# Sums of weights on VectorE, two score chunks in one PSUM bank, and a second buffer for a first block, in a hybrid FoX and mLSTM layer

## The chip, the cores and the metric

The kernel runs on one core of a Trainium2 chip. The time is that of the device, in microseconds (us), for one execution of the whole layer. Three executions of the kernel before took 957.70, 958.07 and 958.45 us; the median is 958.07 us.

## The reference: what is computed

One layer of a decoder trunk, in float32, for 512 tokens with 16 learned meta tokens put before them (528 rows), width 1024. The input is normalised, one projection gives thirteen pieces, and two branches work on them side by side:

```
h = rms_norm(x, g_pre);  z = h @ w_in
fq, fk, fv, ff, fz, mqk, mv, mi, mf, mo, mz, ga, gb = split(z)
# FoX: 8 heads of 128, causal softmax attention with a decay from cumsum(log_sigmoid(ff))
p  = softmax(where(causal, fq.fk * scale + cum[q] - cum[k], -inf))
ya = ((p @ fv) * silu(fz)) @ w_a
# mLSTM: 4 heads, keys of 256, values of 512, chunks of 128, after a causal convolution of mqk
hb = sigmoid(mo) * mlstm_scan(mq, mk, mv, log_i, log_f)
yb = (rms_norm(hb, g_head) * silu(mz)) @ w_b
merged = sigmoid(ga) * ya + sigmoid(gb) * yb
out = x + rms_norm(merged @ w_o, g_post)      # without the 16 meta rows
```

The widths that matter here: fq, fz, ga and gb are 1024 wide each, mz is 2048.

## The kernel before

**Precision.** Every float32 operand of a matmul is split in a high part, rounded to TensorE's fast float32 form, and a low rest. `mm3` (L148 to L151) makes three matmuls of each product: high by high (L149) and the two mixed ones (L150, L151). The high part of a weight is a copy on ScalarE, the low part a subtraction on VectorE: L141 and L143 in `wsplit`, L249 and L251 in `split`. In the profile's names a tile `wq_r` is the raw weight as loaded, `wq_h` and `wq_l` are its two parts.

**Units of seven products.** For fq, fz, ga, gb and mz, 256 output channels at a time, the kernel multiplies a 2 by 2 block form of the weights and of the tokens with seven block products instead of eight (`st_products`, letters X, Y, Z, W for the quarter of two PSUM banks into which a product goes). `st_narrow` prepares the weights of such a unit: the first block by itself (`wXa`, memory `whs`/`wls` in the pool `sums`, one buffer), then two sums in place on the raw weights by GpSimd (L259 and L260, 128 partitions by 512), the split of these (`wXb`), of the second raw tile (`wXc`), two sums by VectorE (L265, L266) and the split of those (`wXd`). The prefix names the unit: `wz10` is the first of the two z units of mLSTM head 1, `wz11` the second, `wfz0`, `wgb1`, `wga2` and `wfq2` are units of FoX. In a unit the products come in this order: X with a, Y and Z with b, W and Y with c, X and Z with d. ScalarE takes snapshots out of the banks between them: L313 after the first Y, L317 after W, L321 after X. VectorE recombines at the end (L324, L325, L327). There are 8 z units, two for each head, and 16 in FoX: four each of fq, fz, ga and gb.

**The order of the program.** For each of four mLSTM heads: the convolution of q and k, the values, the scores (`score_part`: VectorE L727, ScalarE L728, VectorE L730 and L732), the output gate `so`, and the first pair of value chunks (`value_part`, L785 to L806), the first z unit, the second pair of chunks, the second z unit. Head 0 takes `so` as a plain projection ahead of the scores (sigmoids L741), the others as a wide unit behind them (sigmoids L757). The transposes `pht` (L816), which read the normalised chunks (L806), and the products `pyb` of a head come with the next head. Then come four rounds p = 0 to 3 of FoX, each of two heads: fq, fk, then for each head `prob_part` (scores `pl`, softmax), `ptr_part` (transposes, copies L986 and L987) and `fout_part` (L1005), and between them fv in even rounds and one or two gate units: fz and then gb in p = 0 and p = 2, fz and then gb or ga in p = 1 and p = 3. fz ends with a sigmoid and a multiplication (L920, L921), gb and ga with a sigmoid (L927). At the end stand the merge with w_a and the output projection.

**What sets the order.** A scheduler orders the instructions of each engine ahead of the run, from the program's order, the operations' assumed costs and the buffers that are free; each engine then executes its list strictly in that order. Buffers come from pools with a fixed number of turns: four for raw weights, four each for `wXb`, `wXc`, `wXd` and the other split weights together, eight PSUM banks, one for `whs` and `wls`. A tile waits until the last reader of its predecessor in that buffer is done. Loads stand in SyncE's list, and every raw tile is a load of 512 KB.

Of the kernel before, what the change touches and what calls it, by code (L numbers as in the profile page):

```python
# [26 lines left out]
MV = 512  # L27
# [5 lines left out]
C_MO, C_MZ, C_GA, C_GB = 8208, 10256, 12304, 13328  # L33
# [8 lines left out]
OFFA = [0, 144, 416, 816]  # L42
# [11 lines left out]
def tile_hybrid_block(ctx: ExitStack, tc: tile.TileContext, x, meta, norm_pre, norm_post, w_in, b_fox_f,  # L54
# [14 lines left out]
    def psum1(name):  # L69
        return pa.tile([P, 512], F32, tag="pa", name=name)  # L70
# [22 lines left out]

    wk = ctx.enter_context(tc.tile_pool(name="work", bufs=1))
    mw = ctx.enter_context(tc.tile_pool(name="sums", bufs=1))

    def sb(shape, dt, tag, name, pool=None, **kw):

# [143 lines left out]
        TB["b21"] = blk(hh, 1, 0), blk(hl, 1, 0)  # L242
        TB["b22"] = blk(hh, 1, 1), blk(hl, 1, 1)

    def split(src, name, tags=("whi", "wlo"), pool=None, bufs=None):
        kw = {} if bufs is None else {"bufs": bufs}
        shape = [P, src.shape[1], src.shape[2]]
        hi = (pool or wp).tile(shape, F32R, tag=tags[0], name=f"{name}_h", **kw)
        S.activation(hi, src, AF.Copy)  # L249
        lo = (pool or wp).tile(shape, F32R, tag=tags[1], name=f"{name}_l", **kw)  # L250
        V.tensor_tensor(lo, src, f(hi), ALU.subtract)  # L251
        return hi, lo

    def st_narrow(c0, name):

        (r0,), (r1,) = (wload(win, 512 * i, 4, c0, 256, f"{name}{i}")[0] for i in range(2))
        a, b = slice(0, P), slice(P, 2 * P)
        o = {"a11": split(r0[:, :, a], f"{name}a", ("whs", "wls"), mw, 1)}
        G.tensor_tensor(r0[:, :, a], r0[:, :, a], r0[:, :, b], ALU.add)  # L259
        G.tensor_tensor(r0[:, :, b], r0[:, :, b], r1[:, :, b], ALU.add)  # L260
        x, y = split(r0, f"{name}b")
        o["s3"], o["s1"] = (x[:, :, a], y[:, :, a]), (x[:, :, b], y[:, :, b])
        x, y = split(r1, f"{name}c")
        o["a12"], o["a22"] = (x[:, :, a], y[:, :, a]), (x[:, :, b], y[:, :, b])
        V.tensor_tensor(r1[:, :, b], r0[:, :, a], r1[:, :, b], ALU.add)  # L265
        V.tensor_tensor(r1[:, :, a], r1[:, :, a], r1[:, :, b], ALU.add)  # L266
        x, y = split(r1, f"{name}d")
        o["s4"], o["s2"] = (x[:, :, a], y[:, :, a]), (x[:, :, b], y[:, :, b])
        return o
# [18 lines left out]
    def st_products(o, units):  # L288


        begun = set()

        def prod(d, w, t):
            (wh_, wl_), (th, tl) = o[w], TB[t]
            for m, (wz, yx, _, ts) in enumerate(units):
                bank = wz if d in "WZ" else yx
                dst = bank[:, 0:256] if d in "WY" else bank[:, 256:512]
                first = (m, d in "WZ") not in begun
                begun.add((m, d in "WZ"))
# [12 lines left out]
        for wz, yx, snap, _ in units:
            S.activation(snap[:, 0:2], halves(yx), AF.Copy)  # L313
        prod("Z", "s1", "t1")
        prod("W", "a12", "b21")
        for wz, yx, snap, _ in units:
            S.activation(snap[:, 3], wz[:, 256:512], AF.Copy)  # L317
        prod("Y", "a22", "t4")
        prod("X", "s2", "t2")
        for wz, yx, snap, _ in units:  # L320
            S.activation(snap[:, 2], yx[:, 256:512], AF.Copy)  # L321
        prod("Z", "s4", "b22")
        for wz, yx, snap, _ in units:
            V.tensor_tensor(yx[:, 256:512], snap[:, 0], yx[:, 256:512], ALU.subtract)  # L324
            V.tensor_tensor(halves(yx), halves(yx), snap[:, 2:4], ALU.subtract)  # L325
        for wz, yx, snap, _ in units:
            V.tensor_tensor(halves(wz), halves(wz), snap[:, 1:3], ALU.add)  # L327
# [177 lines left out]
    for b in range(NCH):  # L505
# [6 lines left out]
        s0 = NM + b * P  # L512
# [244 lines left out]
                S.activation(dst, units[m][i].rearrange("p (s n) -> p s n", s=2), AF.Sigmoid)  # L757
        return so

    def st_unit(c0, name, room):  # L760

        ps = banks(f"p{name}", 2)
        st_products(st_narrow(c0, f"w{name}"), [(ps[0], ps[1], room.rearrange("p a (b n) -> p (a b) n", b=2), None)])
        return ps

    def mz_part(h, u):
        g = sb([P, 2, SEQ], F32, ("qk1h", "qk1l")[u], f"gz{h}{u}")
        ps = st_unit(C_MZ + h * MV + u * 256, f"z{h}{u}", g)
        for m in range(2):
            S.activation(g[:, m, :], ps[m], AF.Sigmoid)  # L770
        for m in range(2):
            mi = 80 + h * 4 + u * 2 + m
            V.scalar_tensor_tensor(g[:, m, :], ps[m], gc[:, mi:mi + 1], g[:, m, :], ALU.mult, ALU.mult)
        return g
# [165 lines left out]
    def prob_part(p, m, q, k):  # L940

        h = 2 * p + m
        qh, ql = q
        kh, kl = k
        ab = sb([P, NA], F32, "ab", f"ab{h}", gp)
        nc.sync.dma_start(ab, d_na[h:h + 1, :].to_broadcast([P, NA]))
        pn = sb([P, NPACK], F32, "w", f"pn{h}")
        for c in range(NCH):
            kn = NM + (c + 1) * P
            o = OFFA[c] + kn - P  # L950
            G.tensor_tensor(ab[:, o:o + P], ab[:, o:o + P], mask_q, ALU.add)
            lt = sb([P, L], F32, "y", f"lt{h}{c}", bufs=2)
            parts = [(0, kn)] if kn <= 512 else [(0, HL), (HL, kn)]
            mn = line(wk, f"mn{h}{c}", 2, tag="mn", bufs=4)
            for i, (s0, s1) in enumerate(parts):
                ps = psum1(f"pl{h}{c}{i}")
                mm3(ps[:, 0:s1 - s0], qh[:, m, c * P:(c + 1) * P], ql[:, m, c * P:(c + 1) * P],
                    kh[:, m, s0:s1], kl[:, m, s0:s1], True, True)
                V.tensor_tensor_reduce(out=lt[:, s0:s1], in0=ps[:, 0:s1 - s0], in1=ab[:, OFFA[c] + s0:OFFA[c] + s1],
                                       op0=ALU.add, op1=ALU.min, scale=1.0,  # L960
                                       scalar=3e38 if i == 0 else mn[:, 0:1], accum_out=mn[:, i:i + 1])
            li = len(parts) - 1
            rsum = line(wk, f"rsum{h}{c}", 1, tag="r", bufs=4)
            S.activation(lt[:, 0:kn], lt[:, 0:kn], AF.Exp, bias=mn[:, li:li + 1], scale=-1.0, accum_out=rsum)
            V.reciprocal(rsum, rsum)  # L965
            o = OFFP[c]
            G.tensor_scalar(pn[:, o:o + P].rearrange("p (g t) -> p g t", g=4),  # L967
                            lt[:, 0:32].unsqueeze(1).to_broadcast([P, 4, 32]), rsum, None, ALU.mult)
            V.tensor_scalar(pn[:, o + P:o + P + kn - NM], lt[:, NM:kn], rsum, None, ALU.mult)
        return pn  # L970

    def ptr_part(p, m, pn):
        h = 2 * p + m
        pth = sb([P, NCH, SEQ], F32R, "big_h", f"pth{h}")
        ptl = sb([P, NCH, SEQ], F32R, "big_l", f"ptl{h}")
        ptm = sb([P, SEQ], F32R, "ptm", f"ptm{h}", gp)
        pmt = psum1(f"pmt{h}")
        for c in range(NCH):
            o = OFFP[c]
            pt = psum1(f"pt{h}{c}")  # L980
            for j in range(c + 1):
                T.transpose(pt[:, j * P:(j + 1) * P], pn[:, o + P + j * P:o + P + (j + 1) * P], ident)
            T.transpose(pmt[:, c * P:(c + 1) * P], pn[:, o:o + P], ident)
            pv = pt[:, 0:(c + 1) * P].rearrange("p (j t) -> p j t", t=P)
            dst = pth[:, 0:c + 1, c * P:(c + 1) * P]
            S.activation(dst, pv, AF.Copy)  # L986
            V.tensor_tensor(ptl[:, 0:c + 1, c * P:(c + 1) * P], pv, f(dst), ALU.subtract)  # L987
# [28 lines left out]
        return gh, gl  # L1016

    bt = turn_part(*pend)
    gp = ctx.enter_context(tc.tile_pool(name="fox", bufs=1))
    d_yb = [dram.tile([P, 2, SEQ], F32, name=f"d_yb{u}") for u in range(4)]  # L1020
    d_sa = [dram.tile([P, 2, SEQ], F32, name=f"d_sa{u}") for u in range(3)]
    q = fq_part(0)
# [138 lines left out]
```

## Time and profile before

| | us |
|---|---|
| median of three executions | 958.07 |
| the profiled execution | 958.12 |
| its span, first to last instruction | 956.3 |
| TensorE (PE) busy | 915.8 (96%) |
| VectorE (DVE) busy | 649.0 (68%) |
| ScalarE (ACT) busy | 473.9 (50%) |
| GpSimd (POOL) busy | 194.1 (20%) |
| mean granted TensorE clock | 0.999 |

The profiled execution took 1.8 us more than its span. TensorE works almost without a pause, so the times at which it stands and what it then waits for say more than the shares of the other engines. In the views an entry such as "PE pz L149 <- ACT gz L317" says that the matmul of line 149 into tile pz waited for ScalarE's instruction of line 317 on tile gz. In a timeline each row is one instruction or a run of like ones: its start, its length, engine, line, operation, the tile written and those read, shapes, and in brackets the time that the engine stood idle before it with what ended that. Tiles are shown without their numbers: `pz` is any of the z units' banks.

### The profile page before, as it was taken

The page shows a single profiled execution, that of the slowest core. Times are in us where ns is not written, and L with a number is a line of the kernel's source. Part 1 is how long each engine was busy: PE and PEld are TensorE (multiplying, and loading weights), DVE is VectorE, ACT ScalarE, POOL GpSimd, SP SyncE. Part 2 cuts the span into 40 slices and gives each one's busy share as a digit, 9 for nine tenths or more (in the row PEclk, how much of TensorE's full clock was granted, in tenths as well). Part 3 has the DMA queues.
Part 4 walks back from the last instruction along what each step waited for, and adds up shares of the span by engine and source line. Part 5 has one row for each costly group of instructions (what it writes and reads, how often), then busy time and mean ns, then how long its engine had stood idle before and what let it go on. Part 6 is the DMA issues. An engine that isn't in the chain of part 4 may idle for free.

```text
span 956.3 us, 15752 instructions
## 1 busy us (share of the span) xinstructions
PE 915.8 (96%) x6296; PEld 844.5 (88%) x6296; DVE 649.0 (68%) x1080; ACT 473.9 (50%) x818; POOL 194.1 (20%) x222
## 2 busy tenths in 40 slices
PE   8999799999999999999999999989899999899997
PEld 6998799889998899988999988889798899798887
DVE  6988598447686276872768665677774676885633
ACT  5746456435565254662545424455653554773331
POOL 3055100120101211012112114223531233410000
PEclk9999999999999999999999999999999999999999
DMA  7323143203223222322223325224342233248402
GB/s 226 91 82 95 45 129 104 88 23 111 88 90 105 61 81 75 113 77 87 73 61 110 112 88 162 62 79 133 102 155 74 73 90 110 89 167 311 145 23 89
DMA packets 73539, 97.47 MB, mean 102 GB/s; under 512 B 5237, under 2 KB 56533, under 8 KB 73466
## 3 DMA queue, kind: packets, MB, share of 16 engines
q1 hardware_dynamic: 71400, 92.76, 31.7%
q0 software_dynamic: 576, 2.10, 0.6%
q10 hardware_dynamic: 1490, 1.61, 0.5%
q8 instruction: 49, 0.80, 0.3%
q14 instruction: 24, 0.20, 0.1%
HBM read 90.62 MB, written 5.83 MB: 101 GB/s over the span
## 4 chain that ended last, share of the span: by engine, by line
PE 73%; DVE 11%; issue 5%; POOL 5%; ACT 4%; DMA 1%; POOLq 0%; DVEq 0%; ACTq 0%
PE pyb L150 3%; PE pyb L151 3%; PE pyb L149 3%; PE pv L151 3%; PE pv L150 3%; PE pv L149 3%; PE po L149 3%; PE po L151 3%; PE po L150 3%; PE pqk L149 3%; PE pqk L151 3%; PE pqk L150 3%; PE pfk L149 2%; PE pfk L151 2%; PE pfk L150 2%
## 5 line engine op out<-in xcount | busy, mean ns | idle before, releaser
L967 POOL TENSOR_SCALAR pn<-lt,rsum 128x128 f32<-128x128 f32 x32 | 31.1, 972 | 108.6 <-DVE rsum L965 58.6
L150 PE MATMUL pyb<-bl,wb_h 128*128 128x512 f32 x128 | 49.9, 390 | 0.0
L151 PE MATMUL pyb<-bh,wb_l 128*128 128x512 f32 x128 | 49.8, 389 | 0.0
L149 PE MATMUL pyb<-bh,wb_h 128*128 128x512 f32 x128 | 49.8, 389 | 0.0
L150 PE MATMUL pv<-wv_l,hh 128*128 128x512 f32 (+1 forms) x128 | 46.6, 364 | 1.5 <-DVE wv_l L143 1.5
L151 PE MATMUL pv<-wv_h,hl 128*128 128x512 f32 (+1 forms) x128 | 46.4, 363 | 0.0
L149 PE MATMUL pv<-wv_h,hh 128*128 128x512 f32 (+1 forms) x128 | 46.4, 363 | 0.0
L694 DVE SCALAR_TENSOR_TENSOR y<-z,gc,y 128x512 f32<-128x512 f32 (+1 forms) x48 | 36.2, 759 | 2.0 <-ACT y L687 1.3
L149 PE MATMUL pqk<-hh,wq_h 128*128 128x258 f32 x128 | 36.4, 284 | 0.0
L149 PE MATMUL pfk<-hh,wfk_h 128*128 128x264 f32 x128 | 36.4, 284 | 0.0
L149 PE MATMUL pqk<-hh,wk_h 128*128 128x264 f32 x128 | 36.3, 284 | 0.0
L151 PE MATMUL pqk<-hh,wk_l 128*128 128x264 f32 x128 | 36.3, 284 | 0.0
L150 PE MATMUL pfk<-hl,wfk_h 128*128 128x264 f32 x128 | 36.3, 284 | 0.0
L151 PE MATMUL pfk<-hh,wfk_l 128*128 128x264 f32 x128 | 36.3, 283 | 0.0
L150 PE MATMUL pqk<-hl,wk_h 128*128 128x264 f32 x128 | 36.3, 283 | 0.0
L150 PE MATMUL pqk<-hl,wq_h 128*128 128x258 f32 x128 | 36.0, 282 | 0.0
L151 PE MATMUL pqk<-hh,wq_l 128*128 128x258 f32 x128 | 36.0, 282 | 0.0
L150 PEld LDWEIGHTS pv<-wv_l,hh 128*128 128x128 f32 x128 | 24.1, 189 | 5.6 <-DVE wv_l L143 1.7
L151 PEld LDWEIGHTS pyb<-bh,wb_l 128*128 128x128 f32 x128 | 24.0, 188 | 5.0
L149 PEld LDWEIGHTS pyb<-bh,wb_h 128*128 128x128 f32 x128 | 24.0, 188 | 4.9
L150 PEld LDWEIGHTS pyb<-bl,wb_h 128*128 128x128 f32 x128 | 24.0, 188 | 4.9
L149 PEld LDWEIGHTS pv<-wv_h,hh 128*128 128x128 f32 x128 | 24.2, 189 | 3.9
(1806 smaller groups left out, 3662.1 us busy)
## 6 DMA issues: line engine op xcount, KB each, us to landing
wv_r<-in_w_in_dram SPq DMA_DIRECT2D x16, 512.0 KB, 4.5
wo_r<-in_w_in_dram SPq DMA_DIRECT2D x16, 512.0 KB, 4.1
wz_r<-in_w_in_dram SPq DMA_DIRECT2D x16, 512.0 KB, 3.7
wb_r<-in_w_b_dram SPq DMA_DIRECT2D x16, 512.0 KB, 3.4
ab<-d_na SPq DMA_DIRECT2D x8, 672.0 KB, 3.8
wq_r<-in_w_in_dram SPq DMA_DIRECT2D x8, 512.0 KB, 3.6
wk_r<-in_w_in_dram SPq DMA_DIRECT2D x8, 512.0 KB, 3.7
wfq_r<-in_w_in_dram SPq DMA_DIRECT2D x8, 512.0 KB, 3.6
```

Source lines behind the costliest of these rows:

```text
L149: T.matmul(ps, ah, bh, start=start, stop=False, **kw)
L150: T.matmul(ps, ah, bl, start=False, stop=False, **kw)
L151: T.matmul(ps, al, bh, start=False, stop=stop, **kw)
L694: V.scalar_tensor_tensor(y[:, t0:L], z[:, m, t0 + j:L + j], gc[:, j * 16 + mi:j * 16 + mi + 1], y[:, t0:L], ALU.mult, ALU.add)
L967: G.tensor_scalar(pn[:, o:o + P].rearrange("p (g t) -> p g t", g=4), lt[:, 0:32].unsqueeze(1).to_broadcast([P, 4, 32]), rsum, None, ALU.mult)
```

## The change

It has three parts.

1. `st_narrow` is told which engine makes the two sums of L259 and L260. The 16 units of FoX use VectorE, the 8 z units of the mLSTM stay with GpSimd.
2. In `prob_part` the score matmuls of all four chunks of a head are written ahead of the softmax, and the first two chunks go into one PSUM bank, 144 columns of one and 272 of the other behind it. Four banks are used for a head's scores instead of five. In `ptr_part` the copies out of PSUM are written behind all transposes.
3. The first block of the second z unit of each head gets memory of its own, under the name `sg` in the pool `fox`, which is opened at the program's start instead of before FoX. Until then this memory is used by nothing else.

```diff
+    gp = ctx.enter_context(tc.tile_pool(name="fox", bufs=1))
...
-    def split(src, name, tags=("whi", "wlo"), pool=None, bufs=None):
+    def split(src, name, tags=("whi", "wlo"), pool=None, bufs=None, into=None):
...
-        hi = (pool or wp).tile(shape, F32R, tag=tags[0], name=f"{name}_h", **kw)
+        hi = into[0] if into else (pool or wp).tile(shape, F32R, tag=tags[0], name=f"{name}_h", **kw)
         S.activation(hi, src, AF.Copy)
-        lo = (pool or wp).tile(shape, F32R, tag=tags[1], name=f"{name}_l", **kw)
+        lo = into[1] if into else (pool or wp).tile(shape, F32R, tag=tags[1], name=f"{name}_l", **kw)
         V.tensor_tensor(lo, src, f(hi), ALU.subtract)
...
-    def st_narrow(c0, name):
+    def st_narrow(c0, name, adder, into=None):
...
-        o = {"a11": split(r0[:, :, a], f"{name}a", ("whs", "wls"), mw, 1)}
-        G.tensor_tensor(r0[:, :, a], r0[:, :, a], r0[:, :, b], ALU.add)
-        G.tensor_tensor(r0[:, :, b], r0[:, :, b], r1[:, :, b], ALU.add)
+        o = {"a11": split(r0[:, :, a], f"{name}a", ("whs", "wls"), mw, 1, into)}
+        adder.tensor_tensor(r0[:, :, a], r0[:, :, a], r0[:, :, b], ALU.add)
+        adder.tensor_tensor(r0[:, :, b], r0[:, :, b], r1[:, :, b], ALU.add)
...
-    def st_unit(c0, name, room):
+    def st_unit(c0, name, room, adder=V, into=None):
...
     def mz_part(h, u):
         g = sb([P, 2, SEQ], F32, ("qk1h", "qk1l")[u], f"gz{h}{u}")
-        ps = st_unit(C_MZ + h * MV + u * 256, f"z{h}{u}", g)
+        into = None
+        if u:
+            t = sb([P, 2, 4, P], F32R, "sg", f"wz{h}{u}a", gp)
+            into = t[:, 0], t[:, 1]
+        ps = st_unit(C_MZ + h * MV + u * 256, f"z{h}{u}", g, G, into)
...
+        sums = []
         for c in range(NCH):
             kn = NM + (c + 1) * P
             o = OFFA[c] + kn - P
             G.tensor_tensor(ab[:, o:o + P], ab[:, o:o + P], mask_q, ALU.add)
+            for s0, s1 in [(0, kn)] if kn <= 512 else [(0, HL), (HL, kn)]:
+
+                if c != 1:
+                    bank = psum1(f"pl{h}{c}{s0}")
+                ps = (bank[:, 144:512] if c == 1 else bank)[:, 0:s1 - s0]
+                mm3(ps, qh[:, m, c * P:(c + 1) * P], ql[:, m, c * P:(c + 1) * P],
+                    kh[:, m, s0:s1], kl[:, m, s0:s1], True, True)
+                sums.append((c, s0, s1, ps))
...
-            V.tensor_tensor(ptl[:, 0:c + 1, c * P:(c + 1) * P], pv, f(dst), ALU.subtract)
+            pts.append(pt[:, 0:(c + 1) * P].rearrange("p (j t) -> p j t", t=P))
+        for c, pv in enumerate(pts):
```

The order of TensorE's instructions is the same in both. What moves is on the other engines, and three places matter. In the rows the number in front is the row's place in its engine's list; the changed text has other line numbers.

VectorE in mLSTM head 0, between the split of the first z unit's weights (`wz00`) and the head's scores (`w`, `wl`), before:

```order
129 L251 TENSOR_TENSOR wz00c_l<-wz_r_1252,wz00c_h 128x1024
130 L265 TENSOR_TENSOR wz_r_1252<-wz_r_1250,wz_r_1252 128x4x128
131 L266 TENSOR_TENSOR wz_r_1252<-wz_r_1252 128x4x128
132 L251 TENSOR_TENSOR wz00d_l<-wz_r_1252,wz00d_h 128x1024
133 L727 TENSOR_TENSOR w_957<-ps_1120,w_957 128x512
134 L727 TENSOR_TENSOR w_957<-ps_1130,w_957 128x384
135 L730 TENSOR_TENSOR wl_1119<-w_957,wh_1118 128x512
```

and with the change:

```order
129 L252 TENSOR_TENSOR wz00c_l<-wz_r_1255,wz00c_h 128x1024
130 L252 TENSOR_TENSOR wz01a<-wz_r_1428,wz01a 128x512
131 L266 TENSOR_TENSOR wz_r_1255<-wz_r_1253,wz_r_1255 128x4x128
132 L267 TENSOR_TENSOR wz_r_1255<-wz_r_1255 128x4x128
133 L252 TENSOR_TENSOR wz00d_l<-wz_r_1255,wz00d_h 128x1024
134 L728 TENSOR_TENSOR w_960<-ps_1123,w_960 128x512
135 L252 TENSOR_TENSOR wz01b_l<-wz_r_1428,wz01b_h 128x1024
136 L731 TENSOR_TENSOR wl_1122<-w_960,wh_1121 128x512
```

The second z unit's `wz01a` and `wz01b` have come ahead of the scores; before, they stood behind the first pair of value chunks. ScalarE's `wz01b_h` likewise now stands between the sigmoids of `so` (L741 before) and the copies `wh`.

ScalarE in head 1, from the output gate's snapshots to the first z unit's first snapshot (`gz`, L313 before), before:

```order
186 L249 ACTIVATE wz10c_h<-wz_r_2551 128x1024
...
191 L249 ACTIVATE wz10d_h<-wz_r_2551 128x1024
192 L757 ACTIVATE so_2238<-po_0_2239 128x2x256
...
198 L249 ACTIVATE wz11a_h<-wz_r_2723 128x512
199 L313 ACTIVATE gz_2546<-pz_1_2548 128x512
200 L249 ACTIVATE wz11b_h<-wz_r_2723 128x1024
201 L249 ACTIVATE wz11c_h<-wz_r_2725 128x1024
202 L317 ACTIVATE gz_2546<-pz_0_2547 128x256
```

and with the change:

```order
186 L250 ACTIVATE wz11a<-wz_r_2726 128x512
187 L250 ACTIVATE wz10c_h<-wz_r_2553 128x1024
...
192 L250 ACTIVATE wz10d_h<-wz_r_2553 128x1024
193 L250 ACTIVATE wz11b_h<-wz_r_2726 128x1024
194 L758 ACTIVATE so_2240<-po_0_2241 128x2x256
...
200 L314 ACTIVATE gz_2548<-pz_1_2550 128x512
201 L250 ACTIVATE wz11c_h<-wz_r_2728 128x1024
```

The copies of wz11a and wz11b have come ahead of the sigmoids of `so`; only that of wz11c still stands between the two snapshots.

ScalarE in FoX, p = 0, in the fz unit (`yb` and `pfz`) while the weights of the gb unit (`wgb1`) are prepared, before:

```order
475 L313 ACTIVATE yb<-pfz_1_6420 128x512
476 L249 ACTIVATE wgb1b_h<-wgb_r_6589 128x1024
477 L964 ACTIVATE lt_6402,rsum_6414<-lt_6402,mn_6403 128x528
478 L249 ACTIVATE wgb1c_h<-wgb_r_6591 128x1024
479 L317 ACTIVATE yb<-pfz_0_6419 128x256
480 L321 ACTIVATE yb<-pfz_1_6420 128x256
```

and with the change:

```order
475 L314 ACTIVATE yb<-pfz_1_6414 128x512
476 L977 ACTIVATE lt_6404,rsum_6408<-lt_6404,mn_6405 128x528
477 L250 ACTIVATE wgb1b_h<-wgb_r_6583 128x1024
478 L318 ACTIVATE yb<-pfz_0_6413 128x256
479 L250 ACTIVATE wgb1c_h<-wgb_r_6585 128x1024
480 L322 ACTIVATE yb<-pfz_1_6414 128x256
```

The exponential of the softmax stands ahead of wgb1b_h, and the snapshot L317 (now L318) ahead of wgb1c_h.

More of the change, by code (lines that the diff above doesn't have):

```diff
@@ L758, in mo_part @@
         return so
-    def st_unit(c0, name, room):
+    def st_unit(c0, name, room, adder=V, into=None):
         ps = banks(f"p{name}", 2)
-        st_products(st_narrow(c0, f"w{name}"), [(ps[0], ps[1], room.rearrange("p a (b n) -> p (a b) n", b=2), None)])
+        st_products(st_narrow(c0, f"w{name}", adder, into), [(ps[0], ps[1], room.rearrange("p a (b n) -> p (a b) n", b=2), None)])
         return ps
@@ L951, in prob_part @@
             G.tensor_tensor(ab[:, o:o + P], ab[:, o:o + P], mask_q, ALU.add)
+            for s0, s1 in [(0, kn)] if kn <= 512 else [(0, HL), (HL, kn)]:
[5 more added lines that the diff above has]
+                sums.append((c, s0, s1, ps))
+        for c in range(NCH):
+            kn = NM + (c + 1) * P
             lt = sb([P, L], F32, "y", f"lt{h}{c}", bufs=2)
-            parts = [(0, kn)] if kn <= 512 else [(0, HL), (HL, kn)]
             mn = line(wk, f"mn{h}{c}", 2, tag="mn", bufs=4)
[L955 to L959, printed above, removed]
+            parts = [(s0, s1, ps) for c_, s0, s1, ps in sums if c_ == c]
+            for i, (s0, s1, ps) in enumerate(parts):
+                V.tensor_tensor_reduce(out=lt[:, s0:s1], in0=ps, in1=ab[:, OFFA[c] + s0:OFFA[c] + s1],
                                        op0=ALU.add, op1=ALU.min, scale=1.0,
@@ L977, in ptr_part @@
         pmt = psum1(f"pmt{h}")
+        pts = []
         for c in range(NCH):
@@ L983, in ptr_part @@
             T.transpose(pmt[:, c * P:(c + 1) * P], pn[:, o:o + P], ident)
-            pv = pt[:, 0:(c + 1) * P].rearrange("p (j t) -> p j t", t=P)
+            pts.append(pt[:, 0:(c + 1) * P].rearrange("p (j t) -> p j t", t=P))
+        for c, pv in enumerate(pts):
             dst = pth[:, 0:c + 1, c * P:(c + 1) * P]
@@ L1018, in tile_hybrid_block @@
     bt = turn_part(*pend)
-    gp = ctx.enter_context(tc.tile_pool(name="fox", bufs=1))
     d_yb = [dram.tile([P, 2, SEQ], F32, name=f"d_yb{u}") for u in range(4)]
```

## The prediction

> **What bounds the kernel now.** I read the page first, then the clock (0.999, so it plays no part), then TensorE's waits, then the engines' timelines around the long ones.
>
> ```profile
> span 956.3 us, 15752 instructions
> ## 1 busy us (share of the span) xinstructions
> PE 915.8 (96%) x6296; PEld 844.5 (88%) x6296; DVE 649.0 (68%) x1080; ACT 473.9 (50%) x818; POOL 194.1 (20%) x222
> ```
>
> The change leaves every matmul as it is. All that can be won lies in the 956.3 − 915.8 = 40.5 us in which TensorE is idle, and all that can be lost is a longer wait there. TensorE's waits (waiting line and tile, releaser, total in us, times, longest), for 500 to 860 us (FoX), 112 to 525 (mLSTM) and 99 to 103 (head 0's scores):
>
> ```profile
> PE pfz L149 <- ACT yb L317: 6.7, 4, 2.2
> PE pga L149 <- ACT sga L317: 3.6, 2, 2.0
> PE pgb L149 <- DVE yb L921: 3.5, 2, 1.8
> PE pl L149 <- DVE ptl L987: 2.0, 2, 1.0
> PE pgb L149 <- ACT sgb L317: 1.6, 1, 1.6
> PE pl L149 <- DVE mn L959: 1.0, 2, 0.5
> ```
>
> ```profile
> PE pz L149 <- ACT gz L317: 3.5, 7, 0.8
> PE pht L816 <- DVE ht L806: 1.2, 2, 0.6
> PE pz L149 <- ACT gz L313: 0.6, 1, 0.6
> ```
>
> ```profile
> PE ps L149 <- ACT yb L741: 3.2, 1, 3.2
> ```
>
> The L317 and L313 rows are one story: the last products of a seven-product unit write into a PSUM bank of which ScalarE must first have copied the other half. The timelines of ScalarE and GpSimd show why it is late (start, length, engine, line, tiles, idle before it and what ended that), in head 1's z units and in the fz unit of p = 0:
>
> ```profile
> 243.82 1.06 ACT L249 ACTIVATE wz11b_h<-wz_r 128x1024 fp32r<-128x1024 f32 x1 [3.15 <-POOL wz_r L260]
> ```
>
> ```profile
> 620.76 1.06 ACT L249 ACTIVATE wgb1b_h<-wgb_r 128x1024 fp32r<-128x1024 f32 x1 [3.45 <-POOL wgb_r L260]
> ```
>
> ```profile
> 622.45 1.04 ACT L249 ACTIVATE wgb1c_h<-wgb_r 128x1024 fp32r<-128x1024 f32 x1
> 623.39 0.36 ACT L317 ACTIVATE yb<-pfz 128x256 f32<-128x256 f32 x1
> ```
>
> ```profile
> 619.45 1.28 POOL L260 TENSOR_TENSOR wgb_r<-wgb_r,wgb_r 128x512 f32<-128x512 f32 x1
> ```
>
> ScalarE works in order. The copy wX·b (L249) of the *next* unit stands ahead of the snapshot L317 and waits for the GpSimd sums L259 and L260; ScalarE idles 3.15 and 3.45 us, and TensorE waits behind the snapshot.
>
> **The change part by part: the mLSTM.** GpSimd keeps the z units' sums; the second unit's first block gets memory of its own. The new order puts wz?1a and wz?1b ahead of the heads' `so` sigmoids, so at heads 1 to 3 no copy that waits for GpSimd stands ahead of a snapshot. The three mLSTM rows hold 3.5 + 1.2 + 0.6 = 5.3 us in ten places; the two pht waits follow because L806 and its mean square wait for ScalarE in the same stretch. Each wait also costs a slower restart, seen in TensorE's groups for 245 to 262 us, where four matmuls behind a wait take 26 ns more each, 0.10 us a place:
>
> ```profile
> L149 PE MATMUL pz<-hh,wz10d_h 128*128 128x256 f32 x4 | 1.2, 308 | 0.6 <-ACT gz L317 0.6
> L150 PE MATMUL pz<-hl,wz11d_h 128*128 128x256 f32 x4 | 1.1, 282 | 0.0
> ```
>
> Ten places make 1.0, so −6.3 us, which is also the most. The least is the L317 waits alone, −3.5, if L806 and L313 stay. `so` comes a copy (1.06 us) later; L806 and the transposes that read it come long after, so I put that at nothing; without that cover it costs 1.06 at each of three heads.
>
> **Head 0 pays.** There score work stands right behind the moved instructions. Rows of ScalarE, VectorE (two stretches) and GpSimd:
>
> ```profile
> 98.79 1.06 ACT L249 ACTIVATE wz00d_h<-wz_r 128x1024 fp32r<-128x1024 f32 x1 [3.01 <-PE ps L151]
> ```
>
> ```profile
> 97.98 0.69 DVE L266 TENSOR_TENSOR wz_r<-wz_r 128x512 f32<-128x512 f32 x1
> 99.88 1.22 DVE L251 TENSOR_TENSOR wz00d_l<-wz_r,wz00d_h 128x1024 fp32r<-128x1024 f32 x1 [1.20 <-ACT wz00d_h L249]
> ```
>
> ```profile
> 89.05 1.30 DVE L216 TENSOR_TENSOR t4l<-yb,t4h 128x1024 fp32r<-128x1024 f32 x1
> 90.28 2.30 DVE L216 TENSOR_TENSOR t3l<-yb,t3h 128x1024 fp32r<-128x1024 f32 x1
> ```
>
> ```profile
> 89.25 2.25 POOL L259 TENSOR_TENSOR wz_r<-wz_r 128x512 f32<-128x512 f32 x1
> ```
>
> wz01a_l, a 128x512 subtract (0.69 by L266's row), goes ahead of L265 and L266 on VectorE. L266 ended at 98.67 and wz00d_h began at 98.79, so 0.69 − 0.12 = 0.57 us goes onto wz00d_h, the table load, the sigmoids L741 and the `ps` matmuls behind them. wz01b_h (1.06, as wz00d_h) then stands between the sigmoids and the `wh` copies, and wz01b_l (1.22, as wz00d_l) on VectorE ahead of the first `wl`, for which TensorE waits next. The two chains alternate there, so the second need not count in full: 0.57 + 1.06 = 1.6 is the low end, with the 1.22 it is 2.9.
>
> The row of t3l speaks of more. It took 2.30 us beside a GpSimd sum where its twin t4l took 1.30, and the sum took 2.25 against 1.28 undisturbed. The sums of wz01 have to wait for wz01a_l, so they now start just as VectorE does L265 and L266. One such collision adds 1.0, for a high end of 3.9. I take 2.9, near the middle (2.75). The mLSTM gains 6.3 − 2.9 = 3.4 us.
>
> [...]
>
> **FoX.** 16 units × 2 = 32 sums leave GpSimd and come to VectorE at the price of L266's row, 0.69: 22 us, so VectorE goes from 649 to 671 (70%). In fz of p = 0:
>
> ```profile
> 618.93 0.48 DVE L959 CUSTOM_DVE_ANT_0 lt<-pl,ab,mn 128x264 f32<-128x264 f32 x1
> 619.34 0.08 DVE L959 DVE_READ_ACCUMULATOR2_ANT mn<- 128x1 f32 x1
> ```
>
> Two sums behind mn (619.42) end at 619.42 + 1.38 = 620.80; GpSimd's ended at 619.45 + 1.28 = 620.73. The engine itself wins nothing. But a softmax scaling just ahead collided with L259, and without the sum it is shorter:
>
> ```profile
> 617.92 1.09 DVE L969 TENSOR_SCALAR pn<-lt,rsum 128x384 f32<-128x384 f32 x1
> ```
>
> ```profile
> 689.53 0.56 DVE L969 TENSOR_SCALAR pn<-lt,rsum 128x384 f32<-128x384 f32 x1
> ```
>
> So the sums end at 620.3 to 620.8. What wins is the order: the snapshot stands ahead of wgb1c_h now. It ends 1.06 + 0.36 behind the sums, at 621.7 to 622.2 instead of 623.75. TensorE, ready 2.2 ahead of that, at 621.5, waits 0.2 to 0.7 instead of 2.2.
>
> Part of this is handed on, to the next wait: pgb's for L921. Rows of ScalarE, and of VectorE:
>
> ```profile
> 628.16 1.28 ACT L920 ACT_TABLE_LOAD   x1 [0.65 <-DVE pfz L327]
> 629.45 0.60 ACT L920 ACTIVATE yb<-pfz 128x512 f32<-128x512 f32 x1
> ```
>
> ```profile
> 630.08 0.69 DVE L921 TENSOR_TENSOR yb<-pfz,yb 128x512 f32<-128x512 f32 x1 [0.88 <-ACT yb L920]
> ```
>
> From wgb1b_h's end (621.3 to 621.8) VectorE has two 128x1024 subtracts, four 128x512 (two sums, two recombinations) and one 128x256 (half of 0.69 at least): 2.44 + 2.76 + 0.35 = 5.55, less the 0.07 by which neighbours overlap (619.41 against 619.34) at seven steps: 5.1. The table load then begins at 626.4 to 626.9 instead of 628.16, 1.2 to 1.7 earlier, and so does pgb; with a further wait for ScalarE (wgb1c_h) in the chain 0.8. I take 1.2, for p = 0 and again for p = 2 (the pgb row counts two alike).
>
> In p = 1 and 3 the other two of the four pfz waits (6.7 − 2 × 2.2 = 2.3, so 1.1 each) go likewise, and the waits for L987 (2.0 in 2) stay, since its copies are as late as before. The 1.6 for L317 of pgb (p = 1) and the like of pga (p = 3) go. Behind pgb, pfq of p = 2 now takes the bank of pgb_0, free only after the sigmoid:
>
> ```profile
> 697.74 1.28 ACT L927 ACT_TABLE_LOAD   x1 [3.21 <-DVE pgb L327]
> 699.03 0.60 ACT L927 ACTIVATE sgb<-pgb 128x512 f32<-128x512 f32 x1
> ```
>
> ```profile
> 698.17 0.69 DVE L1005 TENSOR_TENSOR yb<-pfo,yb 128x512 f32<-128x512 f32 x1
> ```
>
> pfq began behind L1005, at 698.86. One subtract (1.22) and one sum (0.69) no longer stand ahead of L327, so the sigmoid's end moves from 699.63 to 697.7 to 698.4: 0.5 to 1.2 won, up to 1.7 without a collision like L969's 0.5. I take 1.1 for p = 1. In p = 3 nothing takes that bank, and L1005 moves ahead of the wga2c_l subtract (1.22): 1.3 to 1.9 won, taken 1.6. The first ga unit keeps its 2.0, because there ScalarE waits for a load:
>
> ```profile
> 547.66 0.63 ACT L249 ACTIVATE wgb0a_h<-wgb_r 128x512 fp32r<-128x512 f32 x1 [4.14 <-DMA wgb_r<-in_w_in_dram]
> ```
>
> FoX: 1.2 + 1.2 + 1.1 + 1.6 = 5.1; low 0.8 + 0.8 + 0.5 + 1.3 = 3.4; high 1.7 + 1.7 + 1.7 + 1.9 = 7.0.
>
> **The shared bank.** Chunk 0's first VectorE read now waits for chunk 1's three matmuls too. A matmul 256 wide lasts 0.282 us by the row above and these are 272 wide, so at most some 0.9 us in each of four parts; lt is on TensorE's path only where mn holds pl (two places), hence 0 to 1.8. I take nothing, as the pl waits have the transposes' copies before them.
>
> **Sum.** 958.12 us (1.8 outside the span, 0.05 above the median) − 3.4 − 5.1 = 949.6.
>
> **The rivals.**
> *In FoX the waits only change their name*: table load, sigmoid and L921 hold TensorE as long as before. For it, 3.5 us already ends at L921; against it, VectorE's chain starts earlier. Only 3.4 is won: 954.7.
> *More goes*: FoX's removable L317 waits (6.7 + 1.6 + 1.6 = 9.9) go and nothing is handed on, and head 0 pays 1.6. For it, GpSimd's collisions leave FoX; against it, the table load still stands ahead of L921. 958.1 − 6.3 + 1.6 − 9.9 = 943.5.
> *VectorE becomes FoX's bound*, the slower case: 2 × 0.69 = 1.4 us lies on the path at eight of the sixteen units, those whose waits end in L921, L927 or L1005: +11.0 less 3.4, 965.7; at half of these, 960.2. It decides from the point where p = 0's first L921 ends later than before, counted from the unit's first product. For it, VectorE is at 68% already; against it, it idles 0.88 ahead of L921.
> *The z units don't gain what they should*: wz?1b still waits for sums that now collide, L806 and L313 stay (−3.5), head 0 pays 3.9, and FoX goes as in the first rival: 958.5, no change.
>
> **How the numbers follow.** Forecast 0.44, more 0.18, changed names 0.18, no change 0.08, slower 0.12. The forecast's own bounds are 958.1 − 6.3 + 1.6 − 7.0 = 946.4 and 958.1 − 3.5 + 3.9 − 3.4 = 955.1. The range goes halfway to "more" and past "changed names" with the shared bank's 1.8: 944.5 to 957. A measurement of this kernel tells 0.2% (1.9 us) from no change. Faster: 0.44 + 0.18 + 0.18 = 0.80; same 0.08; slower 0.12.
>
> **What would show it.** Right: no wait of pz at L317 or L313; no gap ahead of wz11b_h; the waits of `ps` and `pnb` near 101 to 111 us longer by 2 to 4 in sum; pfz's wait at most 0.7 in p = 0 and 2, with a longer one of pgb behind it (1.8 + 1.5 to 2.0 − 1.2 to 1.7, so 1.6 to 2.6); the ga wait at 548 still there; GpSimd busy 41 us less (32 × 1.28), VectorE 22 more. Wrong: pgb later after its unit's start than before, so VectorE binds; new waits of pl or pht; or a head 0 that has not moved, so that the moved copies' price was wrong.

## The result, and the profile after

The changed kernel takes 946.18 us (median of four executions, 945.64 to 947.19), the kernel before beside it 958.26 us (957.70 to 959.64). The ratio is 0.9873 with a 95% interval of 0.9856 to 0.989: faster by 12 us, where 8.5 had been forecast. The profiled execution took 945.64 us, with a span of 943.9 us, 12.4 less than before.

From the page of the changed kernel, the engines' busy time:

```profile
PE 916.6 (97%) x6296; PEld 848.3 (90%) x6296; DVE 667.8 (71%) x1112; ACT 476.0 (50%) x818; POOL 148.9 (16%) x190
```

GpSimd lost 45 us and VectorE gained 19 (41 and 22 had been forecast). TensorE's waits after the change, first for FoX (500 to 860 us), then for head 0 (95 to 115 us); lines have moved by 1 to 15:

```profile
PE pgb L150 <- DVE yb L926: 5.3, 2, 2.6
PE pfq L150 <- ACT sgb L932: 1.2, 1, 1.2
PE pfq L150 <- ACT fqs L314: 0.9, 1, 0.9
PE pga L150 <- DVE yb L1020: 0.6, 1, 0.6
PE pga L150 <- ACT sga L318: 0.6, 1, 0.6
PE pga L150 <- DVE mn L972: 0.5, 1, 0.5
PE pgb L150 <- DVE mn L972: 0.4, 1, 0.4
```

```profile
PE ps L150 <- ACT yb L742: 4.5, 1, 4.5
PE pnb L792 <- DVE wl L731: 0.8, 1, 0.8
PE pnb L790 <- ACT wh L729: 0.7, 1, 0.7
```

All the L317 waits of pz and pfz are gone; from 112 to 525 us the row of pfq for fqs L314 is the only one left. Both kinds of pl waits are gone too: those for L987, which had been expected to stay, and those for mn, which turn up at `pgb` and `pga` (0.4 and 0.5). The wait for the fz multiplication (L921, now L926) grew from 3.5 to 5.3 us, and head 0's wait for the sigmoids from 3.2 to 4.5.

Because TensorE's list is the same in both kernels, the start of the same matmul can be compared in the two traces. The last column is what was won or lost since the row above.

| the matmul | before, us | after, us | shift | of this |
|---|---|---|---|---|
| head 0, first matmul of the first z unit (wz00a) | 112.06 | 115.47 | +3.4 | +3.4 |
| head 3, first `pht` | 515.10 | 510.71 | −4.4 | −7.8 |
| first `pyb` behind the first ga unit | 550.14 | 545.53 | −4.6 | −0.2 |
| p = 0, gb's third product (wgb1c) | 635.15 | 630.35 | −4.8 | −0.2 |
| first matmul of p = 2 (wfq2a) | 698.91 | 690.62 | −8.3 | −3.5 |
| p = 2, gb's third product (wgb3c) | 775.51 | 767.23 | −8.3 | 0.0 |
| ga unit 3, last weights (wga3d) | 858.34 | 846.32 | −12.0 | −3.7 |

FoX gives 7.4 us from 550 on, but in other rounds than forecast: p = 0 and p = 2 give next to nothing, p = 1 and p = 3 give 3.5 and 3.7. In p = 0 the reason stands in the engines' busy time by stretches (start and end; length; busy time of TensorE, weight loads, VectorE, ScalarE, GpSimd, each with its instructions; granted clock; DMA share; GB/s):

```profile
core 0: us, PE busy (x) PEld busy (x) DVE busy (x) ACT busy (x) POOL busy (x), PEclk, DMA share, GB/s
618.00:621.00 3.00, 3.00 (x23) 2.79 (x22) 2.96 (x6) 0.52 (x1) 2.85 (x4) 1.00 0.13 19
621.00:624.50 3.50, 0.86 (x9) 0.65 (x7) 2.64 (x5) 3.29 (x7) 0.19 (x1) 1.00 0.54 154
624.50:628.00 3.50, 3.50 (x18) 3.50 (x18) 3.44 (x8) 2.06 (x5) 0.00 (x0) 0.54 0.40 136
```

Behind the wait of 2.6 us TensorE's clock is granted at 0.54 in the mean of 3.5 us; it is 0.50 from 624.80 to 628.22. The matmuls of gb's first product show it, after the change and before:

```profile
L152 PE MATMUL pgb<-hh,wgb1a_l 128*128 128x256 f32 x4 | 1.7, 413 | 0.0
```

```profile
L151 PE MATMUL pgb<-hh,wgb1a_l 128*128 128x256 f32 x4 | 1.1, 280 | 0.0
```

From its start to that of the next product, gb's first product takes 1.49 us before and 2.43 after, its second 2.74 and 3.42: 1.6 us lost. In p = 2 it is 1.4 (1.49 against 2.70, and 2.73 against 2.97).

### The profile page after: what moved, and what is told of

Read it like the earlier page. It is cut to its first block, busy times and chain, and to the rows that moved or that the text cites. A ratio compares the mean times of both kernels' runs of the same rounds, so it can differ in the third digit from the quotient of the medians.

```text
span 943.9 us, 15725 instructions
## 1 busy us (share of the span) xinstructions
PE 916.6 (97%) x6296; PEld 848.3 (90%) x6296; DVE 667.8 (71%) x1112; ACT 476.0 (50%) x818; POOL 148.9 (16%) x190
## 4 chain that ended last, share of the span: by engine, by line
PE 76%; DVE 11%; ACT 6%; issue 2%; POOL 2%; DMA 2%; POOLq 0%; DVEq 0%; ACTq 0%; SPq 0%
PE pyb L152 3%; PE pyb L150 3%; PE pyb L151 3%; PE pz L150 3%; PE pz L151 3%; PE pz L152 3%; PE pqk L150 3%; PE pqk L152 3%; PE pqk L151 3%; PE pv L152 3%; PE pv L150 3%; PE pv L151 3%; PE po L152 2%; PE po L151 2%; PE po L150 2%
## 5 line engine op out<-in xcount | busy, mean ns | idle before, releaser
L980 POOL TENSOR_SCALAR pn<-lt,rsum 128x128 f32<-128x128 f32 x32 | 28.4, 891 | 136.2 <-DVE rsum L978 99.5
L845 DVE TENSOR_TENSOR yb<-pyb,yb 128x512 f32<-128x512 f32 x24 | 16.5, 688 | 17.4 <-PE pyb L152 17.4
```

The lines of the kernel that those rows point to most:

```text
L845: V.tensor_tensor(dst, ps[i], dst, ALU.add)
```

## The experiments

The times of the kernel before, beside these runs, have medians of 958.51 to 959.14 us (958.26 beside the changed kernel); each ratio is against those of its own session.

**The three parts, each by itself.**

```diff
# adds_only: the kernel before with
-        G.tensor_tensor(r0[:, :, a], ...);  G.tensor_tensor(r0[:, :, b], ...)
+        adder.tensor_tensor(r0[:, :, a], ...);  adder.tensor_tensor(r0[:, :, b], ...)   # V in FoX, G for mz
```

> Only the first part: FoX units' sums on VectorE, scores in five banks, no second buffer. Own theory (each part works at its own place): the snapshot waits of pfz, pgb and pga (6.7 + 1.6 + 1.6 us before) go, pgb's wait for the fz multiplication grows and takes them back in p = 0 and 2, the pl waits (2.0 + 1.0 us) stay; about 4.4 us won, 953.7 us. Rival (the sums only pay with the freed bank, because the pl waits take over what they free): about 1 us won, 957. Rival of the prediction (VectorE binds): slower, 960 or more.

Measured: 947.65 us (947.33 to 948.22), ratio 0.9889 (0.9874 to 0.9903). The sums alone win 11 us, two and a half times what the own theory gave them. Part of it is that the pl waits, which were to stay, shrink to 0.5 us without any freed bank. The waits in FoX:

```profile
PE pgb L149 <- DVE yb L921: 5.1, 2, 2.6
PE pfq L149 <- ACT fqs L313: 1.8, 1, 1.8
PE pfq L149 <- ACT sgb L927: 1.2, 1, 1.2
PE pz L149 <- ACT gz L313: 0.7, 1, 0.7
PE pga L149 <- DVE yb L1005: 0.5, 1, 0.5
PE pl L149 <- DVE ptl L987: 0.5, 2, 0.3
```

All three theories miss, the slower one most. Another part lies at the border of the mLSTM: FoX's first sums no longer stand in GpSimd's list, and `pht` of head 3 starts 1.1 us earlier than before.

```diff
# bank_only: the kernel before with the new prob_part and ptr_part
```

> Only the second part: two score chunks in one bank, copies behind all transposes. Own theory: the two pl waits for the transposes' copies (2.0 us) and the two for mn (1.0 us) go, as they have in the changed kernel, and nothing else moves: 3.0 us won, 955.1 us. Rival (a freed bank only hands the wait on to pgb): at most 0.5 us won, 957.6. The prediction's step said that these waits stay: 958.

Measured: 959.97 us (958.11 to 962.02, ten executions), ratio 1.0012 (1.0 to 1.0024): nothing, or a trifle slower. The 3.0 us that the own theory gave to the bank are refuted. The waits show that names changed and the sum stayed:

```profile
PE pfz L149 <- ACT yb L317: 6.7, 4, 2.2
PE pgb L149 <- DVE yb L921: 3.2, 3, 1.7
PE pga L149 <- ACT sga L317: 2.6, 2, 1.7
PE pga L149 <- DVE yb L1015: 1.8, 1, 1.8
PE pgb L149 <- ACT sgb L317: 1.7, 1, 1.7
PE pga L149 <- DVE yb L921: 1.2, 1, 1.2
PE pl L149 <- DVE ptl L997: 1.2, 2, 0.6
```

The pl waits fall from 3.0 to 1.2 us; 1.8 turn up at `pga` for L1015, a bank that is now taken in another turn, and 1.2 for L921.

```diff
# buffer_only: the changed kernel with the old prob_part and ptr_part, and
-    def st_unit(c0, name, room, adder=V, into=None):
+    def st_unit(c0, name, room, adder=G, into=None):
```

> Only the third part: own memory for the first block of the second z unit. Own theory: head 0 loses about 3.2 us, the waits of pz and pht go for 7.8 us, and FoX is as before: 4.5 us won, 953.6 us. Rival (the moved sums of GpSimd collide with VectorE and the gain shows only together with the other parts): 1.5 us won, 956.6. In head 0 TensorE's wait for the sigmoids is expected at 4.5 us, against 3.2 before.

Measured: 952.97 us (952.77 to 953.27), ratio 0.9944 (0.9929 to 0.9959), 0.6 us below what the own theory gave. TensorE's waits in head 0 (95 to 115 us), and from there to 525 us:

```profile
PE ps L150 <- ACT yb L742: 4.7, 1, 4.7
PE pnb L790 <- ACT wh L729: 0.7, 1, 0.7
```

```profile
PE pfq L150 <- ACT fqs L314: 0.9, 1, 0.9
PE pht L821 <- DVE ht L811: 0.8, 1, 0.8
```

Both sides are as the theory has them: 4.7 us of wait at head 0, and no wait of pz in any head; of the pht waits one of 0.8 us is there. The three parts by themselves add up to 11.1 + 5.8 − 1.2 = 15.7 us, together they give 12.1. The 1.1 us at head 3's end, which the sums win by themselves, are among those that the buffer wins too. And p = 0 gives 1.6 us to the sums by themselves (their shift goes from −1.6 at `pfvm` to −3.2 at wgb1c), where the changed kernel gets nothing: in the trace of adds_only the clock stays up there. The rest was not taken apart.

**The buffer without head 0.**

```diff
# buffer_heads_1_3: the changed kernel with
-        if u:
+        if u and h:
```

> The changed kernel with the second buffer for heads 1 to 3 alone; head 0 takes its second first block from the old buffer. Own theory: head 0's loss of 3.2 us goes, and the 0.7 us that its z unit won come back: 946.2 - 3.2 + 0.7 = 943.7 us. Rival (head 0's lateness is caught up later by waits that shrink): 946.2, no change against the changed kernel.

Measured: 941.80 us (940.70 to 942.84), ratio 0.9823 (0.9805 to 0.9841): 4.4 us below the changed kernel, more than expected. The wait for the sigmoids is 2.8 us. In the two traces (945.64 and 942.84 us) the same matmuls come 2.4 us earlier from head 1 on and 2.8 at the end, about the 2.5 of the own theory; the rest of the 4.4 does not show in them. Head 0's loss is real and is not caught up later.

**The changed kernel without the shared bank, and the last without it.**

```diff
# adds_and_buffer: the changed kernel with the old prob_part and ptr_part
# buffer_1_3_no_bank: the same, and the buffer for heads 1 to 3 alone
```

> The changed kernel without its second part: five banks of scores, copies chunk by chunk. Own theory (the sums alone have taken the pl waits away, the shared bank adds nothing): 946.2 us, within 0.7 of the changed kernel. Rival (the freed bank is what takes the last 0.5 us of pl waits away): 946.7 to 947.2. Rival (the shared bank costs, as it did by itself, 1.2 us): 945.

> The buffer for heads 1 to 3 alone and the sums on VectorE, without the shared bank. Own theory (head 0's 4.4 us and the bank's nothing add up): 941.8 us, as with the bank. Rival (the bank costs 1 us): 940.8. Rival (the bank serves the pl waits): 942.5.

Measured: 946.42 us (943.83 to 948.19, ratio 0.9867, 0.985 to 0.9884) against the changed kernel's 946.18, and 943.11 us (939.76 to 943.78, ratio 0.9837, 0.9823 to 0.985) against 941.80. The first is the own theory's number; the second lies 1.3 above it, with intervals that overlap. No effect of the bank can be told in either pair.

**What pushes head 0 back.**

```diff
# z01_on_vector: the changed kernel with
-        ps = st_unit(..., f"z{h}{u}", g, G, into)
+        ps = st_unit(..., f"z{h}{u}", g, V if (h, u) == (0, 1) else G, into)
```

> The changed kernel with one difference: in head 0 the second z unit's two sums are made by VectorE (behind its own L267) and not by GpSimd. Own theory (GpSimd's sums collide with VectorE's L267, which took 1.64 us instead of 0.69, and push the sigmoids and TensorE's ps matmuls back): L267 takes 0.69, wz00d_h begins 0.95 earlier, TensorE's wait of 4.5 us shrinks to 3.5; 946.2 - 1.0 = 945.2 us, and 944 if the clock then stays up. Rival (L267 is slow for another reason): no change, 946.2. Rival (1.4 us more on VectorE ahead of wz00d_l costs more than the collision): 946.6 or more.

Measured: 944.58 us (943.08 to 946.13), ratio 0.984 (0.9824 to 0.9857). Timelines of the changed kernel (VectorE, GpSimd, ScalarE), then VectorE in this one:

```profile
98.23 1.64 DVE L267 TENSOR_TENSOR wz_r<-wz_r 128x512 f32<-128x512 f32 x1
```

```profile
97.73 1.59 POOL L260 TENSOR_TENSOR wz_r<-wz_r 128x512 f32<-128x512 f32 x1 [4.23 <-DVE wz01a L252]
```

```profile
99.98 1.06 ACT L250 ACTIVATE wz00d_h<-wz_r 128x1024 fp32r<-128x1024 f32 x1 [4.44 <-DVE wz_r L267]
```

```profile
98.79 0.69 DVE L267 TENSOR_TENSOR wz_r<-wz_r 128x512 f32<-128x512 f32 x1
```

L267 takes 1.64 us beside GpSimd's sum and 0.69 without it: the collision is there and costs 0.95. The scheduler put one of the two new VectorE sums ahead of L267, so wz00d_h starts only 0.4 us earlier (99.59) and TensorE's wait shrinks from 4.5 to 3.9. In this trace nothing comes of it: the first z unit begins at 115.89 instead of 115.47 us, behind 10.2 us of granted clock 0.50 (103.63 to 113.87), and with 946.13 us it is the longest of the four executions, 0.5 above the profiled one of the changed kernel. That the median moves by 1.6 is not explained by it, and the two kernels' times overlap.

**The halved clock.**

```diff
# keep_busy: the changed kernel with, in ptr_part behind the transposes of a chunk,
+            if m == 1 and p % 2 == 0:
+                for j in [j for _ in range(2) for j in range(c + 1)]:
+                    T.transpose(pt[:, j * P:(j + 1) * P], pn[:, o + P + j * P:...], ident)
```

> The changed kernel, in which the second head of p = 0 and p = 2 makes each transpose of its weights three times over (same data, same place), so that TensorE works about 2 us longer ahead of its wait for the fz multiplication. Own theory (TensorE's clock is halved for some 3 us because it did next to nothing for 2.6 us, and that costs 1.6 us in p = 0 and 1.2 in p = 2): the wait ends at the same point, the clock stays at 1.00, 946.2 - 2.8 = 943.4 us. Rival (the slow matmuls behind the wait have another cause, such as the loads that run there): 946.2, the slow stretch stays. Rival (the copies behind the transposes come later and hold the path): 947 or more.

Measured: 943.68 us (943.38 to 944.00), ratio 0.9841 (0.9827 to 0.9854); 943.4 was expected. More work on TensorE makes the kernel 2.5 us faster. Its stretches around the same place:

```profile
621.00:624.50 3.50, 3.50 (x34) 3.38 (x31) 2.64 (x5) 3.25 (x4) 0.75 (x2) 1.00 0.55 153
624.50:628.00 3.50, 3.06 (x27) 2.97 (x26) 3.44 (x8) 2.62 (x7) 0.00 (x0) 1.00 0.52 152
```

The clock stays at 1.00 while the loads run as before (0.52 and 152 GB/s), so these are not the cause. In the trace the two places give 1.6 and 1.4 us, as the halved clock had cost, and 0.8 is lost at the first ga unit. That the wait's length alone doesn't decide shows in adds_only, whose waits in p = 0 and p = 2 are alike (2.5 and 2.6 us). In the traces the clock changes only at points that lie 3.41 us or a multiple of that apart (shown in the last section). Between such points adds_only looks like this: the step with most of the wait and the step behind it, in p = 0 and then in p = 2:

```profile
623.81:627.22 3.41, 1.43 (x14) 1.19 (x11) 2.55 (x4) 3.21 (x4) 1.04 (x3) 1.00 0.53 157
627.22:630.63 3.41, 2.88 (x25) 2.91 (x26) 3.38 (x8) 2.59 (x7) 0.00 (x0) 1.00 0.51 155
760.35:763.76 3.41, 0.79 (x7) 0.58 (x6) 2.55 (x5) 3.21 (x8) 0.00 (x0) 1.00 0.55 167
763.76:767.17 3.41, 3.41 (x18) 3.41 (x17) 3.35 (x8) 1.65 (x4) 0.00 (x0) 0.50 0.24 85
```

The first wait (625.24 to 627.75) is cut by the point at 627.22, its step holds 1.43 us of work, and the clock stays up. The second lies in one step as a whole, with 0.79 us of work, and the next step runs at 0.50.

**An early table load, and the best of all.**

```diff
# early_table: the changed kernel with
+    def early_table(name):
+        dry = line(wk, f"dry{name}", 1, tag="ss", bufs=8)
+        pin(S.activation(dry, mhalf, AF.Sigmoid))
...
+        early_table(f"fz{p}")                # in fz_part, behind st_unit
```

> The changed kernel with a sigmoid of one column for ScalarE behind the snapshots of each fz unit, so that its table load (1.28 us) no longer stands behind the recombination. Own theory: pgb's wait of 2.6 us in p = 0 and 2 shrinks by 1.28 and the clock no longer drops, 1.28 + 1.4 us for each: 946.2 - 5.4 = 940.8 us. Rival (the load is hidden, but the order moves elsewhere and pgb's wait ends in something else, such as the multiplication or the copies of the transposes): 943 to 946.

Measured: 942.24 us (940.82 to 942.70), ratio 0.9823 (0.981 to 0.9836), between the two theories. In p = 0 the load now runs in a gap of ScalarE and the multiplication comes 1.2 us earlier in the trace; pgb waits 1.7 us instead of 2.6, gb's third product starts 2.9 us earlier, and the clock stays at 1.00 from 500 to 900 us. In p = 3 the same edit moved wga2b_h behind other work, and TensorE's waits there (815 to 835 us) show what that costs:

```profile
PE pga L150 <- ACT wga2b_h L250: 1.5, 1, 1.5
```

```diff
# best_early_table: buffer_heads_1_3 with the early load, where p < 3
# best_and_busy: that, and the transposes of keep_busy
```

> The buffer for heads 1 to 3 alone, and the early table load in p = 0, 1 and 2, not in p = 3, where it moved other work into TensorE's way for 3 us. Own theory (the gains stand at different places and add up): 941.8 - 2.9 (p = 0) - 1.4 (p = 1) - 2.2 (p = 2) = 935.3 us. Rival (the early load's order in p = 3 was not the cause of the loss there): 938.

> As the kernel before it in this list, with the transposes of p = 0 and 2 made three times over. Own theory (pgb's wait is 1.7 us by now, too short for the clock to drop): no gain, 935.3 us, or some tenths more. Rival (the clock still drops in some executions): 934.5 and a smaller spread.

Measured: 937.07 us (935.91 to 937.70), ratio 0.9766 (0.9751 to 0.978), and 937.73 us (936.56 to 938.77), ratio 0.9774 (0.9759 to 0.9788). The first beats both kernels; it is 1.8 us above the sum of the single gains and 0.9 below the rival's number. The additional transposes bring nothing once the wait is 1.7 us; in both traces the clock is 1.00 from 500 to 900 us.

## Why the prediction was right, and where it was not

**Direction and place were right.** The snapshots had been late because ScalarE waited for GpSimd's sums, and all waits that the first section put down to this are gone. The size was short: the mLSTM gave 4.4 us where 3.4 had been forecast, FoX 7.4 instead of 5.1, and 946.18 us lie 0.2 below 946.4, the lower of the forecast's own bounds. That FoX came so near is in part luck, since two errors stood against each other: p = 0 and p = 2 gave 2.2 us less than forecast, p = 1 and p = 3 gave 4.5 more.

**The mLSTM** was forecast at 6.3 won and 2.9 lost, and gave 7.8 and 3.4. The term that was mis-sized is what a wait costs. The sum took the ten waits at the length shown, 5.3 us, and added the restart. But a wait is counted from the end of the last matmul, and here matmuls of 0.28 us start every 0.12 us. The end of head 1's first z unit, before:

```profile
245.17 0.28 PE L150 MATMUL pz<-t2l,wz10d_h 128*128 128x256 f32 x1
245.28 0.28 PE L151 MATMUL pz<-t2h,wz10d_l 128*128 128x256 f32 x1
246.15 0.39 PE L149 MATMUL pz<-hh,wz10d_h 128*128 128x256 f32 x1 [0.59 <-ACT gz L317]
```

The last start comes 0.87 us behind the one ahead of it instead of 0.12, so a wait of 0.59 costs 0.75, which is 0.16 more than its length. All ten places of the trace before show the same 0.16 (the shortest wait, 0.23 us, has 0.51 between the starts, the longest, 0.81, has 1.09), which makes 1.6; with 5.3 and the restart's 1.0 that is 7.9, against 7.8 measured. 6.3 had been called the most; it was not.

**Head 0** lost 3.4 us, where 2.9 had been forecast and 3.9 was the high end. The collision of GpSimd's sums with VectorE that the price of 2.9 left out is there in full (0.95 us at L267: 1.64 beside GpSimd's sum, 0.69 without it in z01_on_vector). The `ps` matmuls behind the sigmoids start 1.2 us later (103.09 against 101.90), between the 0.57 forecast without a collision and the 1.5 (0.57 + 0.95) with one. The other 2.2 us come with the second chain and with two stretches of granted clock 0.50 (102.56 to 105.98 and 109.39 to 112.80), which the forecast did not have. How they divide between the two was not tried, so the nearness of 2.9 and 3.4 is in part luck. The clock alone need not cost that much: buffer_heads_1_3 runs at 0.50 from 103.05 to 109.87, and its first z unit begins 0.3 us later than that of the kernel before (112.36 against 112.06).

**p = 0 and p = 2** were each forecast at 1.2 and gave 0.2 and nothing. The steps themselves held: no pfz wait is left, the table load moved from 628.16 to 621.74, which is 1.4 beyond the shift of 5.0 that TensorE's list had by then (589.58 to 584.59 at `pfvm`), against 1.2 to 1.7 forecast, and pgb waits 2.6 (1.6 to 2.6 forecast). By the starts of the same matmuls, p = 0 wins 2.3 us at pfz and gives 0.9 back at pgb. What the sum lacked is the clock, of which the first sentence of the prediction says that it "plays no part". The kernel before was read in an execution with a mean clock of 0.999, in which TensorE ran at 1.00 from 12 us on to the end of its work; in the trace of the changed kernel 1.6 and 1.4 us went into matmuls at half speed. Most other executions of the kernel before have a mean clock of 0.989 to 0.997, so its clock falls in places too; where, no trace shows. keep_busy gets 2.5 of these 3.0 back.

**p = 1 and p = 3** were forecast at 1.1 and 1.6 and gave 3.5 and 3.7. Two steps failed. The first is "the waits for L987 (2.0 in 2) stay, since its copies are as late as before". They are not. ScalarE's timeline in p = 1 before, where the copy wgb2d_h stands ahead of the transposes' copies `pth` and waits 2.41 us for VectorE:

```profile
678.53 1.06 ACT L249 ACTIVATE wgb2d_h<-wgb_r 128x1024 fp32r<-128x1024 f32 x1 [2.41 <-DVE wgb_r L266]
679.50 0.53 ACT L986 ACTIVATE pth<-pt 128x128 fp32r<-128x128 f32 x2
```

and after, where three of these copies come first and wgb2d_h much later:

```profile
671.55 1.25 ACT L1001 ACTIVATE pth<-pt 128x128 fp32r<-128x128 f32 x3 [1.15 <-PE pt L996]
673.26 1.28 ACT L925 ACT_TABLE_LOAD   x1 [0.45 <-DVE pfz L328]
```

```profile
678.85 1.05 ACT L250 ACTIVATE wgb2d_h<-wgb_r 128x1024 fp32r<-128x1024 f32 x1
```

With the sums on VectorE the scheduler moved wgb2d_h back; the prediction looked at that place's snapshots and not at what stood ahead of `pth`. adds_only has this move and nearly no pl waits, bank_only has neither the move nor the gain. By the starts of the same matmuls, the pl waits that went are worth 1.8 us in each of the two rounds, of which 0.5 comes back at the next wait for mn. That the move itself is the cause, and not the earlier sums, was not tried by itself.

The second step is the sigmoid behind pgb, which ends p = 1 by freeing pfq's bank. The prediction had it end 1.2 to 1.9 us earlier than 699.63. It now ends at 690.57, and since p = 1 began 4.8 us earlier, that is 4.3 earlier on the old scale:

```profile
689.97 0.60 ACT L932 ACTIVATE sgb<-pgb 128x512 f32<-128x512 f32 x1
```

What brought VectorE's recombination ahead of it forward by more than the one subtract and one sum was not taken apart, nor were the 0.8 us of p = 3 that the pl waits leave over.

**The shared bank** was put at nothing, and it is nothing: 1.0012 (1.0 to 1.0024) by itself, 946.42 against 946.18 within the whole.

**The first ga unit** was to keep its 2.0 us. It keeps 0.6, but 0.9 turns up at the fq unit ahead of it and the sum is the same to 0.2 us. Its wait ends with a load, and the load came earlier by about what the mLSTM gave: wgb0a_h, which waits for it, starts at 543.05 instead of 547.66 us, 4.6 earlier. What the fq unit waits is therefore missing from the wait at ga.

**The rivals.** "More goes" came nearest in its sum (943.5), though not by its mechanism: the waits were handed on, in part to a slow clock, and others went instead. VectorE as the bound is refuted: adds_only wins 11 us with all 32 sums on it.

## What to carry to other kernels

When work moves between engines, the scheduler may move what stands around it: look in the new list for what stands ahead of every instruction that TensorE waits for, not only at the step that was edited. Lengths of waits don't add up in a straight line: each of the ten of the mLSTM cost 0.16 us more than its shown length here, besides a restart slower by 0.10 (head 1), and behind waits of 2.6 and 4.5 us of the changed kernel TensorE ran at a granted clock of 0.50, where the kernel before stayed at 1.00 behind one of 3.2. And an edit that is good in nine places can be taken out at the tenth (head 0, or the early table load in p = 3), which here brought another 4 to 9 us.

## What the runs showed of the hardware that was not expected

TensorE's granted clock moved in steps of 3.41 us. In the 13 traces, from 13 us on and up to the last 8 us of each, every stretch at 0.50 lasts 3.41 (the changed kernel, 102.56 to 105.98), 6.83 (buffer_heads_1_3, 103.05 to 109.87) or 10.24 us (z01_on_vector, 103.63 to 113.87), and the points at which the clock changes lie a multiple of 3.41 us apart: in the changed kernel 102.56 and 624.80 are 153 steps of 3.413 us apart. Where these points lie against the program differed between the traces: taken back in such steps to the start of the span, they lie at 0.16 us in the changed kernel, at 1.29 in the kernel before and at 2.58 in adds_only.

What TensorE did between two such points goes with the clock of the next step. Of the steps at full clock in these traces, all 20 with at most 1.35 us of busy time were followed by 0.50 (in the changed kernel those of 0.00, 0.77 and 1.00 us, from 99.15, 621.39 and 757.92 on, so such a step need not be idle), and none with more than 2.1 us was. Between 1.4 and 2.1 us both happened: 1.43 us left the clock up in adds_only, all of it transposes, and 1.80 us in the changed kernel did not. So the busy time as shown is not all that counts, and what else does stays open.

So a wait of 2.6 us can be followed by half speed where one of 3.2 us is not. In head 0 of the kernel before, the wait from 98.7 to 101.9 us is cut at 100.28 (an estimate: 250 steps of 3.413 us back from the clock's change at 953.61):

```profile
96.86:100.28 3.42, 1.82 (x15) 1.68 (x13) 2.15 (x4) 1.47 (x2) 0.00 (x0) 1.00 0.30 69
100.28:103.69 3.41, 1.63 (x6) 1.05 (x6) 1.89 (x3) 3.40 (x7) 0.00 (x0) 1.00 0.64 198
```

In the changed kernel the wait of 4.5 us fills a whole step, and the step of 1.80 us behind it is followed by half speed again:

```profile
99.15:102.56 3.41, 0.00 (x0) 0.00 (x0) 2.21 (x3) 2.55 (x3) 1.77 (x2) 1.00 0.52 154
102.56:105.98 3.42, 2.89 (x7) 1.90 (x7) 0.93 (x2) 3.31 (x6) 0.00 (x0) 0.50 0.51 153
105.98:109.39 3.41, 1.80 (x9) 1.18 (x9) 3.29 (x9) 1.03 (x3) 0.00 (x0) 1.00 0.00 0
109.39:112.80 3.41, 3.41 (x18) 3.41 (x17) 1.83 (x6) 0.63 (x1) 0.10 (x1) 0.50 0.00 0
```

The mean clock of an execution says little by itself: single executions of the kernel before had 0.989 to 0.999 with times of 956.57 to 960.2 us, in no order with it.
